# Another place in SBUF for x, and direct products of 512 columns cut in two

## The chip, the cores and the metric

The kernel runs on one core of one Trainium2 chip. A NeuronCore has TensorE (matmuls, with its own queue of weight loads), VectorE, ScalarE, GpSimd (POOL) and SyncE, which issues most DMAs. The metric is the device time of one execution in microseconds. The time before is 1766.88 us, the median of three runs (1766.7 to 1767.4).

## The reference

Two layers work on 512 tokens of width 1024, in float32. Each has an FFN, a mixer and a second FFN, and each of the three ends in a layer norm over the residual:

```python
for l in range(DEPTH):
    x = layer_norm(DEEPNORM_ALPHA * x + 0.5 * swiglu_ffn(x, ffn1_w_gu[l], ffn1_w_down[l]), ln1_g[l], ln1_b[l])
    x = layer_norm(DEEPNORM_ALPHA * x + hybrid_mixer(x, w_in[l], w_out[l], attn_sinks[l],
                                                     rope_cos, rope_sin, ret_cos, ret_sin), ln2_g[l], ln2_b[l])
    x = layer_norm(DEEPNORM_ALPHA * x + 0.5 * swiglu_ffn(x, ffn2_w_gu[l], ffn2_w_down[l]), ln3_g[l], ln3_b[l])
```

`swiglu_ffn` multiplies x by a 1024 x 5632 matrix, gates one half of the result with the SiLU of the other, and multiplies by a 2816 x 1024 matrix. `hybrid_mixer` projects x to queries, keys, values and gates, runs a windowed softmax attention over one half of the heads and a chunked retention over the other, and projects the result back.

## The kernel before

Every float32 product is made of three reduced-precision ones. `split` writes the rounded value (`hi`, ScalarE, L168) and the rest (`lo`, VectorE, L169) of an operand; `mm3` (L183 to L185) issues hi x hi, hi x lo and lo x hi into the same bank of PSUM. The second argument of `mm3` is the stationary operand, the third the moving one. In the profile a matmul is named out<-moving,stationary: `ps<-xh,uh` streams xh against weights uh.

x lies transposed in `xh` and `xl` (128 partitions, 8 blocks k of 512 tokens each). The weights arrive in two `raw` buffers of 8 KB per partition and are cut into units of 128 x 1024, `uh` and `ul`, six buffers each; `Weights` hands them out in order.

An FFN has eleven column pairs. Pairs 2 to 10 are `glu7`: seven products in place of eight by sums of quarters, so one pass has 72 matmuls with x as moving operand (`xb`) and 96 with sums of x as moving operand (`Th`, `Tl`, made once per FFN by `sums_of_x`), all of 256 columns. Pairs 0 and 1 are direct products through `proj` and `projs`: most are called for 256 tokens, the last two of pair 1 for all 512. Then the second matrix of the FFN is applied with tokens as output rows: `seventh` and `down` take parts of h, which `operand` splits into the room of xh and xl, as stationary operand and stream 512 columns of a unit. The last pair of h lies in `hr`, with units of its own at the tail.

The mixer projects with `emit_T` (256 tokens, the last call 512), `proj_tok` (x stationary, 512 columns of a unit streamed) and, for the retention, `projs` over 512 tokens. Attention and retention are tasks in Python generators that `step` runs between the products; `proj` yields where a step may come: behind half of the k blocks and at the end if it is called for 512 tokens, at the end alone otherwise. So TensorE's order is fixed when the program is written.

Tiles lie in pools, one pool behind the other, each tile padded to a multiple of 32 bytes. In the program before, `base` holds ident (512 bytes per partition, byte 2176), mhalf (32 bytes), xh (byte 2720), xl (19104) and Y (35488). Modulo 256 the last three are at 160. The raw buffers begin at 51872 (160) and the units at 68256 (160); each unit has 4096 bytes, and its eight blocks of 512 bytes lie at 160 too. Behind the units lies `small` (960 bytes in all: three st of 64, three mv, ve and rs of 32 each, and others), then at 118368 the pools of the FFN or the mixer: hT at 96, S and R at 96, Th at 179808 and Tl at 196192, both at 96, hr and the tail's units at 96; the mixer's tiles from qk on at 32.

Of the kernel before, what the change touches and what calls it, by code (L numbers as in the profile page):

```python
# [7 lines left out]
F32 = mybir.dt.float32  # L8
# [7 lines left out]
SEQ = 512  # L16
D = 1024
DFF = 2816
P = 128
KC = D // P  # L20
# [26 lines left out]
class Weights:  # L47


    def __init__(self, T, items):  # L50
        self.T, self.items = T, items
        self.emitted = self.taken = self.out = 0
        self.ready = []
        self.raws = {}
        self.last = {raw: i for i, (raw, _, _, _) in enumerate(items)}
# [44 lines left out]
class Trunk:  # L100
    def __init__(self, tc, ctx):
        self.tc, self.nc = tc, tc.nc
        self.n = 0
        self.now = 0
        self.pin = True
        self.tasks = []
        self.later = []
        self.pace = None
        self.halves = 2
        nc = self.nc  # L110
        self.base = ctx.enter_context(tc.tile_pool(name="base", bufs=1))
        self.rawp = ctx.enter_context(tc.tile_pool(name="rawp", bufs=2))
        self.unit = ctx.enter_context(tc.tile_pool(name="unit", bufs=UBUFS))
        self.small = ctx.enter_context(tc.tile_pool(name="small", bufs=3))
        self.psum = ctx.enter_context(tc.tile_pool(name="psum", bufs=8, space=PSUM))
        self.ident = self.base.tile([P, P], F32, name="ident")
        make_identity(nc, self.ident)
        self.mhalf = self.base.tile([P, 8], F32, name="mhalf")
        nc.vector.memset(self.mhalf, -0.5)
        self.xh = self.base.tile([P, KC, SEQ], F32R, name="xh")  # L120
        self.xl = self.base.tile([P, KC, SEQ], F32R, name="xl")
        self.Y = self.base.tile([P, NT, D], F32, name="Y")
# [320 lines left out]
    def proj(self, out, u, t0, t1):  # L443
        hv, lv = u
        for k in range(KC):
            self.mm3(out, (hv[:, k, :], lv[:, k, :]),
                     (self.xh[:, k, t0:t1], self.xl[:, k, t0:t1]), k == 0, k == KC - 1)
            if k == KC - 1 or (k == KC // 2 - 1 and t1 - t0 == SEQ):
                yield

    def projs(self, *args):
        for _ in self.proj(*args):
            self.step()

    def proj_tok(self, out, us, t):
        ts = slice(t * P, (t + 1) * P)
# [36 lines left out]
    def norm(self, t, halves, gb, out=None, delay=4, scale=(ALPHA, ALPHA)):  # L493
        nc = self.nc
        g, b = gb
        y = self.Y[:, t, :]
        st = self.small.tile([P, 2, 6], F32, tag="st", name=self.nm("st"))
        for h in range(2):
            hs = slice(h * 512, (h + 1) * 512)
            nc.vector.scalar_tensor_tensor(out=y[:, hs], in0=y[:, hs], scalar=scale[h], in1=halves[h],  # L500
                                           op0=ALU.mult, op1=ALU.add)
            nc.vector.bn_stats(out=st[:, h, :], in_=y[:, hs])
        mv = self.small.tile([P, 2], F32, tag="mv", name=self.nm("mv"))
        nc.vector.bn_aggr(out=mv, in_=st)
        ve = self.small.tile([P, 1], F32, tag="ve", name=self.nm("ve"))
        nc.vector.tensor_scalar_add(ve, mv[:, 1:2], LN_EPS)
        rs = self.small.tile([P, 1], F32, tag="rs", name=self.nm("rs"))
        nc.gpsimd.tensor_tensor(out=rs, in0=ve, in1=self.mhalf[:, 0:1], op=ALU.pow)
        nc.vector.scalar_tensor_tensor(out=y, in0=y, scalar=mv[:, 0:1], in1=g, op0=ALU.subtract, op1=ALU.mult)
        parts = [slice(0, D)] if out is None else [slice(0, 512), slice(512, D)]  # L510
        for hs in parts:
            nc.vector.scalar_tensor_tensor(out=y[:, hs], in0=y[:, hs], scalar=rs, in1=b[:, hs],
                                           op0=ALU.mult, op1=ALU.add)
            if out is not None:
                nc.sync.dma_start(out[t * P : (t + 1) * P, hs], y[:, hs])
        if out is None:
            self.pend.append(self.spawn(self.y_to_xT(t), delay))
# [670 lines left out]
```

## Time and profile before

| | |
|---|---|
| median of 3 runs | 1766.88 us |
| span of the profiled execution | 1765.1 us |
| TensorE busy | 1752.7 us (99%), 11930 matmuls |
| VectorE busy | 1414.9 us (80%) |
| ScalarE busy | 928.1 us (53%) |
| POOL busy | 182.9 us (10%) |

The profiled execution has a span, from the first to the last instruction, of 1765.1 us; the median of the runs is 1.8 us above it. Matmuls are pipelined: the durations in the profile overlap, so the sum over the groups is well above the span, and the time that a matmul takes of TensorE is seen in the distance of two starts in the timeline.

### The profile page before, as it was taken

How to read it: one execution, taken by the hardware profiler on the slowest of the kernel's cores; microseconds unless marked ns; L12 is line 12 of the kernel's file. 1: busy time of each engine (PE TensorE's matmuls, PEld its weight loads, DVE VectorE, ACT ScalarE, POOL GpSimd, SP SyncE). 2: the span in 40 equal slices, each digit the busy share in tenths (PEclk: the TensorE clock that was granted, in tenths of full speed). 3: DMA queues.
4: the chain of work that ended last, by engine and by line, in shares of the span. 5: the costliest groups of instructions: out<-in, count | busy, mean ns of one | idle time of the engine just before them, and what ended most of it. 6: DMA issues, size and time to landing. Idle time of an engine off the chain costs nothing.

```text
span 1765.1 us, 29166 instructions
## 1 busy us (share of the span) xinstructions
PE 1752.7 (99%) x11930; PEld 1600.5 (91%) x11930; DVE 1414.9 (80%) x1975; ACT 928.1 (53%) x1456; POOL 182.9 (10%) x152
## 2 busy tenths in 40 slices
PE   9999999999999999999999999999999999999998
PEld 9999988887789999998899999889877899999886
DVE  7888888856767888878888888888567587888887
ACT  5455556378712455555535555554795234555561
POOL 0000022111111000014000000311011110000131
PEclk9999999999999999999999999999999999999999
DMA  6234389422222243369423334982233122334891
GB/s 191 97 96 133 131 202 199 131 85 88 73 79 72 74 137 102 97 208 214 140 68 99 121 96 147 211 203 91 85 95 96 48 95 97 97 96 132 211 218 48
DMA packets 163765, 216.34 MB, mean 123 GB/s; under 512 B 5168, under 2 KB 116528, under 8 KB 163632
## 3 DMA queue, kind: packets, MB, share of 16 engines
q1 hardware_dynamic: 141872, 172.55, 30.5%
q0 software_dynamic: 21760, 41.95, 13.1%
q8 instruction: 93, 1.52, 0.3%
q14 instruction: 40, 0.33, 0.1%
HBM read 212.38 MB, written 2.10 MB: 122 GB/s over the span
## 4 chain that ended last, share of the span: by engine, by line
PE 90%; issue 6%; DMA 1%; DVE 1%; POOL 1%; ACT 0%; SPq 0%; POOLq 0%; DVEq 0%
PE ps L183 29%; PE ps L185 29%; PE ps L184 29%; PE ps L476 1%; DMA raw<-in_ffn_w_gu_dram 1%; POOL sw L959 1%; PE ps L1067 1%; PE ps L1015 0%; PE ps L1029 0%; PE ps L1063 0%; PE ps L1050 0%; DMA retS<-c_retS_dram 0%; ACT sw L957 0%; DVE ul L169 0%; PE ps L1007 0%
## 5 line engine op out<-in xcount | busy, mean ns | idle before, releaser
L183 PE MATMUL ps<-xh,uh 128*128 128x256 f32 (+1 forms) x1616 | 482.2, 298 | 0.0
L185 PE MATMUL ps<-xh,ul 128*128 128x256 f32 (+1 forms) x1616 | 479.3, 297 | 1.0 <-DVE ul L169 0.9
L184 PE MATMUL ps<-xl,uh 128*128 128x256 f32 (+1 forms) x1616 | 478.5, 296 | 0.3 <-DVE xl L169 0.3
L168 ACT CAST uh<-raw 128x1024 fp32r<-128x1024 f32 (+1 forms) x274 | 237.1, 886 | 245.6 <-PE ps L184 140.1
L169 DVE TENSOR_TENSOR ul<-raw,uh 128x1024 fp32r<-128x1024 f32 (+1 forms) x274 | 273.3, 1013 | 62.2 <-ACT uh L168 61.6
L183 PE MATMUL ps<-Th,uh 128*128 128x256 f32 x1152 | 319.1, 277 | 0.0
L184 PE MATMUL ps<-Tl,uh 128*128 128x256 f32 x1152 | 318.7, 277 | 0.0
L185 PE MATMUL ps<-Th,ul 128*128 128x256 f32 x1152 | 318.3, 276 | 0.0
L185 PEld LDWEIGHTS ps<-xh,ul 128*128 128x128 f32 x1616 | 307.9, 191 | 10.1 <-DVE ul L169 1.6
L183 PEld LDWEIGHTS ps<-xh,uh 128*128 128x128 f32 x1616 | 307.9, 191 | 9.7 <-issue 1.6
L184 PEld LDWEIGHTS ps<-xl,uh 128*128 128x128 f32 x1616 | 308.0, 191 | 7.9 <-DVE xl L169 0.5
L183 PE MATMUL ps<-uh,xh 128*128 128x512 f32 x720 | 283.4, 394 | 0.5 <-ACT xh L168 0.5
L185 PE MATMUL ps<-uh,xl 128*128 128x512 f32 x720 | 280.8, 390 | 0.0
L184 PE MATMUL ps<-ul,xh 128*128 128x512 f32 x720 | 280.3, 389 | 0.0
L168 ACT CAST uh<-S 128x1024 fp32r<-128x1024 f32 x144 | 151.1, 1049 | 149.0 <-PE ps L184 145.2
L169 DVE TENSOR_TENSOR ul<-S,uh 128x1024 fp32r<-128x1024 f32 x144 | 175.9, 1222 | 60.1 <-ACT uh L168 59.5
L184 PEld LDWEIGHTS ps<-Tl,uh 128*128 128x128 f32 x1152 | 216.7, 188 | 0.0
L183 PEld LDWEIGHTS ps<-Th,uh 128*128 128x128 f32 x1152 | 216.6, 188 | 0.0
L185 PEld LDWEIGHTS ps<-Th,ul 128*128 128x128 f32 x1152 | 216.4, 188 | 0.0
L389 POOL DMA_DIRECT2D R<-in_ffn_w_down_dram x80 | 97.1, 1217 | 1020.7 <-DVE ul L169 930.0
L169 DVE TENSOR_TENSOR ul<-R,uh 128x1024 fp32r<-128x1024 f32 x120 | 145.1, 1221 | 25.8 <-ACT uh L168 25.7
L183 PEld LDWEIGHTS ps<-uh,xh 128*128 128x128 f32 x720 | 135.2, 188 | 30.1 <-issue 1.6
(143 smaller groups left out, 2362.4 us busy)
## 6 DMA issues: line engine op xcount, KB each, us to landing
raw<-in_ffn_w_gu_dram SPq DMA_DIRECT2D x86, 1024.0 KB, 5.5
R<-in_ffn_w_down_dram POOLq DMA_DIRECT2D x80, 512.0 KB, 7.6
raw<-in_w_in_dram SPq DMA_DIRECT2D x18, 1024.0 KB, 5.2
R<-in_ffn_w_down_dram SPq DMA_DIRECT2D x16, 1024.0 KB, 6.3
raw<-in_ffn_w_down_dram SPq DMA_DIRECT2D x12, 1024.0 KB, 7.2
R<-in_ffn_w_down_dram SPq DMA_DIRECT2D x8, 512.0 KB, 4.3
raw<-in_w_in_dram SPq DMA_DIRECT2D x8, 512.0 KB, 6.1
raw<-in_w_out_dram SPq DMA_DIRECT2D x8, 512.0 KB, 6.4
```

What stands on the lines that cost most here:

```text
L168: a = self.nc.scalar.copy(hi, src)
L169: b = self.low = self.nc.vector.tensor_sub(lo, src, hi.bitcast(F32))
L183: keep(mm(out, ah, bh, start=start, stop=False, **kw))
L184: keep(mm(out, ah, bl, start=False, stop=False, **kw))
L185: keep(mm(out, al, bh, start=False, stop=stop, **kw))
L389: self.nc.gpsimd.dma_start(src, rows(i, j, g * 2, 2), accum_op=ALU.add))
L476: nc.tensor.transpose(b[:, c * P : (c + 1) * P], src[:, c * P : (c + 1) * P], self.ident)
L959: nc.gpsimd.tensor_mul(sw[:, :n], sw[:, :n], S)
L1067: ins = nc.tensor.matmul(ob[:, o0 : o0 + HD], ST[h][:, n, :], vr[:, n, p * P + h * HD : p * P + (h + 1) * HD], start=n == 0, stop=n == 0 o ...
```

## The change

Three tiles of 64 bytes are added to `base` ahead of xh; `norm` uses them in turn for its statistics, in place of tiles from `small`. A pool of one 64-byte tile is put between the raw buffers and the units. In `small`, st goes, ve becomes the third element of mv, and one tile of 32 bytes is added. The two new filler tiles are set to zero on GpSimd at the start. `proj` yields at its end alone, and `projs` calls it for 256 tokens at a time, with a step behind each.

```diff
         self.rawp = ctx.enter_context(tc.tile_pool(name="rawp", bufs=2))
+        self.near = ctx.enter_context(tc.tile_pool(name="near", bufs=1))
+        nc.gpsimd.memset(self.near.tile([P, 16], F32, name="apart"), 0.0)
         self.unit = ctx.enter_context(tc.tile_pool(name="unit", bufs=UBUFS))
         self.small = ctx.enter_context(tc.tile_pool(name="small", bufs=3))
         self.psum = ctx.enter_context(tc.tile_pool(name="psum", bufs=8, space=PSUM))
+        nc.gpsimd.memset(self.small.tile([P, 8], F32, tag="behind", name="behind", bufs=1), 0.0)
         self.ident = self.base.tile([P, P], F32, name="ident")
...
         nc.vector.memset(self.mhalf, -0.5)
+        self.stats = [self.base.tile([P, 2, 8], F32, name=f"st{i}") for i in range(3)]
+        self.norms = 0
         self.xh = self.base.tile([P, KC, SEQ], F32R, name="xh")
...
-            if k == KC - 1 or (k == KC // 2 - 1 and t1 - t0 == SEQ):
-                yield
-
-    def projs(self, *args):
-        for _ in self.proj(*args):
-            self.step()
+        yield
+
+    def projs(self, out, u, t0, t1):
+        for t in range(t0, t1, SEQ // 2):
+            for _ in self.proj(out[:, t - t0 : t - t0 + SEQ // 2], u, t, t + SEQ // 2):
+                self.step()
...
-        st = self.small.tile([P, 2, 6], F32, tag="st", name=self.nm("st"))
+        st = self.stats[self.norms % 3][:, :, :6]
+        self.norms += 1
...
-        mv = self.small.tile([P, 2], F32, tag="mv", name=self.nm("mv"))
-        nc.vector.bn_aggr(out=mv, in_=st)
-        ve = self.small.tile([P, 1], F32, tag="ve", name=self.nm("ve"))
+        mv = self.small.tile([P, 3], F32, tag="mv", name=self.nm("mv"))
+        ve = mv[:, 2:3]
+        nc.vector.bn_aggr(out=mv[:, :2], in_=st)
```

## Rows read from the trace of the kernel before

**Rows 1.** The page: span, TensorE's busy time, the chain by engine.
```profile
span 1765.1 us, 29166 instructions
...
PE 1752.7 (99%) x11930; PEld 1600.5 (91%) x11930; DVE 1414.9 (80%) x1975; ACT 928.1 (53%) x1456; POOL 182.9 (10%) x152
...
PE 90%; issue 6%; DMA 1%; DVE 1%; POOL 1%; ACT 0%; SPq 0%; POOLq 0%; DVEq 0%
```

**Rows 2.** Waits of TensorE, first and last of six: us in total, times, longest.
```profile
PE ps L468 <- POOL ident masks.py:199: 1.4, 1, 1.4
...
PE ps L184 <- DVE xl L169: 0.3, 1, 0.3
```

**Rows 3.** Groups by form on TensorE: shapes xcount | busy us, mean ns | idle.
```profile
L183 PE MATMUL ps<-xh,uh 128*128 128x256 f32 x1408 | 398.5, 283 | 0.0
...
L183 PE MATMUL ps<-Th,uh 128*128 128x256 f32 x1152 | 319.1, 277 | 0.0
...
L183 PE MATMUL ps<-uh,xh 128*128 128x512 f32 x720 | 283.4, 394 | 0.5 <-ACT xh L168 0.5
...
L183 PE MATMUL ps<-xh,uh 128*128 128x512 f32 x208 | 83.6, 402 | 0.0
```

**Rows 4.** One pass of glu7: us, busy of PE, PEld, DVE, ACT, POOL, PEclk, DMA.
```profile
111.62:131.14 19.52, 19.52 (x170) 19.52 (x170) 16.90 (x26) 10.62 (x18) 0.00 (x0) 1.00 0.35 109
```

**Rows 5.** Timeline of TensorE in that pass (start us, us), x before, T between.
```profile
113.20 0.29 PE L183 MATMUL ps<-Th,uh 128*128 128x256 f32 x1
...
113.56 0.28 PE L183 MATMUL ps<-Th,uh 128*128 128x256 f32 x1
...
115.94 0.28 PE L183 MATMUL ps<-xh,uh 128*128 128x256 f32 x1
```

**Rows 6.** Timeline of TensorE, a stretch on x alone.
```profile
12.30 0.28 PE L183 MATMUL ps<-xh,uh 128*128 128x256 f32 x1
...
16.26 0.28 PE L183 MATMUL ps<-xh,uh 128*128 128x256 f32 x1
```

**Rows 7.** Timeline of TensorE, 512 columns, x stationary, then hr stationary.
```profile
312.40 0.39 PE L185 MATMUL ps<-uh,xl 128*128 128x512 f32 x1
...
314.44 0.39 PE L185 MATMUL ps<-uh,xl 128*128 128x512 f32 x1
314.67 0.39 PE L183 MATMUL ps<-uh,hr 128*128 128x512 f32 x1
...
315.59 0.39 PE L184 MATMUL ps<-ul,hr 128*128 128x512 f32 x1
...
319.44 0.39 PE L183 MATMUL ps<-uh,hr 128*128 128x512 f32 x1
```

**Rows 8.** Timeline of TensorE, 512 columns behind a block of transposes.
```profile
329.66 0.40 PE L185 MATMUL ps<-uh,xl 128*128 128x512 f32 x1
329.90 0.39 PE L183 MATMUL ps<-uh,xh 128*128 128x512 f32 x1
...
331.27 0.39 PE L183 MATMUL ps<-uh,xh 128*128 128x512 f32 x1
```

**Rows 9.** Timeline of the start: a constant's memset, the second half's transposes.
```profile
0.24 0.10 POOL L1174 MEMSET const-float32-0.0<- 128x1 f32 x1 [0.24 <-issue]
0.27 0.10 POOL L1174 MEMSET const-float32-1.0<- 128x1 f32 x1
...
5.83 0.55 PE L476 MATMUL ps<-ident,Y 128*128 128x128 f32 x3 [0.30 <-DMA Y<-in_x_dram]
```

**Rows 10.** Timeline of TensorE, its longest idle behind the start.
```profile
23.07 0.39 PE L185 MATMUL ps<-xh,ul 128*128 128x256 f32 x1 [0.70 <-DVE ul L169]
```

**Rows 11.** Groups by form on VectorE: the splits of 128 x 1024.
```profile
L169 DVE TENSOR_TENSOR ul<-raw,uh 128x1024 fp32r<-128x1024 f32 x166 | 201.7, 1219 | 45.5 <-ACT uh L168 44.9
L169 DVE TENSOR_TENSOR ul<-S,uh 128x1024 fp32r<-128x1024 f32 x144 | 175.9, 1222 | 60.1 <-ACT uh L168 59.5
```

**Rows 12.** Groups by form on TensorE in the first 26.3 us.
```profile
L183 PE MATMUL ps<-xh,uh 128*128 128x256 f32 x41 | 11.8, 287 | 0.0
```

## The prediction

> **What bounds the kernel now.** I read the head of the page first: the span is 1765.1 us, TensorE is busy for 99% of it, and 90% of the chain that ended last runs through TensorE [rows 1]. Then the waits of TensorE: six kinds, 4.2 us in all, the longest of them the start of the program [rows 2]. So no other engine and no transfer holds this kernel back for long. TensorE always has a next matmul, and the time is the sum of the distances from one matmul's start to the next one's start. I call that distance the pitch. The durations in the groups by form [rows 3] are no pitch (a 256-column matmul is listed with 283 ns, and its successor starts long before that); a pitch is read from the timeline, as the difference of two starts divided by the matmuls between them.
>
> The timeline gives three pitches. A locked stretch on Th and Tl has 21 pitches from 113.56 to 115.94, so 113.3 ns each [rows 5]. A stretch on xh and xl has 33 from 12.30 to 16.26, so 120.0 ns [rows 6]. Both are 256 columns, the same weight units, the same three products of mm3, both back to back. What differs is where the moving operand lies: T at 96 modulo 256 bytes, x at 160, where the weight units are too. The third pitch, 512 columns of a unit with x (or hr) as stationary operand, is 227 ns (312.40 to 314.67, ten) or 226.5 ns (315.59 to 319.44, seventeen) [rows 7]. In all of these moving and stationary operand have the same offset: units and x both 160, the tail's units and hr both 96.
>
> A change of operand needs some matmuls to settle: the first three on T take 0.36 us, still 120 each, before the pitch falls to 113.3 [rows 5]. So a single pitch behind a change tells little of where the stream settles.
>
> **The change part by part.** *Placement.* Three 64-byte statistics tiles in base move xh, xl, Y and the raw buffers up by 192 bytes, to 96 modulo 256; 64 more bytes in front of the units put those back at 160. In `small` 192 + 96 bytes go and 32 come, so 256 less: what lies behind it (hT, S, T, all of the mixer) stays at its byte. After the change a product on x has the relation that T has now: moving 96, stationary 160.
>
> *256-column products on x.* There are 3 x 1408 = 4224 [rows 3]. 36 passes of glu7 (nine in each of four FFNs) hold 72 each beside 96 on T; one pass takes 19.52 us [rows 4]. With all 168 at 113.3 ns it takes 19.04 us, so 0.48 us less; times 36 that is 17.3 us. This includes T's settling, which has no cause any more when x and T lie alike. Outside the passes are 4224 - 2592 = 1632. Of these 41 + 2 x 40 = 121 start in the first 26.3 us [rows 12], where TensorE runs into weights that are still arriving (0.70 us at 23.07, behind a split) [rows 10]; faster matmuls only wait longer there, so I count nothing for them. 1511 x 6.7 ns = 10.1 us. Together 27.4 us.
>
> *What hides behind TensorE now.* In a pass VectorE is busy for 16.90 and ScalarE for 10.62 of 19.52 us [rows 4]. Both still fit into 19.04 us with 2.1 us to spare, so the splits don't become the bound. The raw buffers' new offset costs their readers nothing: VectorE's split takes 1219 ns from raw at 160 and 1222 ns from S at 96, each with units at 160 [rows 11].
>
> *512 as twice 256.* 3 x 208 = 624 direct products [rows 3] become 1248 of 113.3 ns: 226.6 ns in place of 226.5 to 227, so nothing. (What stays is a weight load more per pair, which TensorE hides at 113.3 ns already on T.) The tasks that are hung between are stepped once behind each half, as now behind half of the 24 matmuls: at the same times. The consumers (rotate, gate) read the whole bank after both halves, and the unit is released there, as before.
> [...]
>
> *512-column products with x as stationary operand.* The change doesn't name them, yet it moves one of their operands: in the seventh and proj_tok, 3 x 720 = 2160 matmuls [rows 3] stream a unit at 160 against x at 96. The trace has this relation only in single pitches at the border to hr, 0.23 us like the rest (314.44 to 314.67) [rows 7]. Bounds: below, the 6.7 ns between 120.0 and 113.3 could come off here too, 2160 x 6.7 = 14.4 us less; above, the mean of seven pitches behind a block of transposes, (331.27 - 329.66) / 7 = 230 ns [rows 8], 3.3 ns more than the settled pitch, 7 us more. I take zero: the settled pitch is 226.5 to 227 ns at two different offsets, and it equals two of the undisturbed 113.3, as if the pair that disturbs at 256 columns had room to spare at 512.
>
> *Small things.* Two memsets on POOL now precede the identity. The constants' memsets start 0.03 us apart and take 0.10 us; the first x block's second half of transposes waits for its transfer at 5.83 us [rows 9], so 0.1 to 0.2 us of delay is covered there, and if it weren't, it is 0.2 us. norm issues the same instructions; its ve now lies in mv's tile, and no new wait on another engine follows, since POOL reads ve alone and VectorE only reads mv behind it. The 192 transposes of Y (eight for each of 24 blocks) get their stationary operand at 96 too; at 6.7 ns each way that is 1.3 us more or less, which I leave at zero.
>
> *Sum.* The profiled execution has a span of 1765.1 us, 1.8 us under the median of 1766.88, so what lies around the span stays 1.8 us. 1766.9 - 27.4 = 1739.5 us.
>
> **The rivals.**
> *Stationary x gains too.* The extra time of a pitch would be a cost of each weight load against its stream, 6.7 ns whatever the columns; then 512 at unlike offsets settles at 220. [...] Against it: no settled 512 stretch under 226.5. Price -14.4 us: 1725 us.
> *Stationary x loses some.* The reversed relation (moving 160, stationary 96) isn't T's. If it holds the stream at the 230 of [rows 8] or a little over, it costs 7 to 15 us: 1747 to 1755 us.
> *Slower.* The single pitch of 0.24 us that stands in the same rows (329.66 to 329.90) [rows 8] becomes the settled one for the 2160, and then some: the break-even is 27.4 / 2160 = 12.7 ns, so a pitch of 239.4. At 240 the time is 1768; at 247, three steps of 6.7 over today's, it is 1783 us. Against it: no pitch in an undisturbed stretch stays there.
> *The change doesn't do what it says.* T may be faster for another reason than its offset: it lies near the upper end of SBUF, is read with 1024 bytes from one k to the next where x has 2048, and is written once per FFN. Then all of x stays at 120.0 and the time is 1766 to 1767 us.
> [...]
>
> **How the numbers follow.** Forecast (1736 to 1743 us) 50%; stationary x gains (1725) 15%; it loses some (1744 to 1760) 23%; the offset isn't the cause (1766 to 1767) 8%; slower (1771 and up) 4%. About 0.2%, 3.5 us, is what a measurement of this kernel can tell from no change. So faster 0.88, same 0.08, slower 0.04. The range reaches from the lower rival, 1724, to the upper part of the third case, 1756; outside are the last two cases and a little of the third.
>
> **What the profile after would show.** The 256-column form of xh,uh has 1824 instructions in place of 1408 (1408 + 2 x 208), the 512-column form on x as moving operand is gone, and TensorE counts 11930 + 624 = 12554 matmuls. A pass of glu7 takes 19.04 us; no settling shows between x and T, 21 pitches taking 2.38 us wherever they are counted. The 2160 matmuls with x stationary stand at 226 to 227 ns, which is the number to look at first if the total is off: each ns there is 2.2 us. A pass that stays at 19.52 means that the offset isn't what separates x from T. A pass between the two with TensorE idle would mean that the splits bind, against my step on VectorE.

## The result and the profile after

| | before | after |
|---|---|---|
| median | 1767.07 us (1766.7 to 1767.4) | 1779.33 us (1776.0, 1776.0, 1782.6, 1783.4) |
| ratio | | 1.0071, 95% interval 1.0052 to 1.0090 |
| profiled execution | span 1765.1 us | 1776.04 us, span 1774.3 us |
| TensorE busy, matmuls | 1752.7 us, 11930 | 1759.4 us, 12554 |

The forecast was 1739.5 us, 1724 to 1756. The change makes the kernel slower, and its runs stand on two levels some 7 us apart, where those of before agree within 0.7 us.

Page of after, its head (compare [rows 1]); then groups by form on TensorE (compare [rows 3]):

```profile
span 1774.3 us, 30416 instructions
...
PE 1759.4 (99%) x12554; PEld 1629.4 (92%) x12554; DVE 1416.0 (80%) x1975; ACT 928.3 (52%) x1456; POOL 181.6 (10%) x154
```
```profile
L188 PE MATMUL ps<-xh,uh 128*128 128x256 f32 x1824 | 513.4, 281 | 0.9 <-DVE b L988 0.7 <-ACT uh L173 0.2
...
L188 PE MATMUL ps<-Th,uh 128*128 128x256 f32 x1152 | 322.3, 280 | 0.0
...
L188 PE MATMUL ps<-uh,xh 128*128 128x512 f32 x720 | 285.2, 396 | 0.5 <-ACT xh L173 0.5
```

TensorE is still busy for 99%, with the 1824 and 12554 instructions that were forecast. But T, which the change doesn't touch, has gone up: 319.1 to 322.3 us. So most of the added time is pitch, in the sense of the prediction. Next, one pass of glu7 in each of the four FFNs of after (FFN 1 to 4, as they run; windows: stretch and its length, TensorE busy and its matmuls, granted clock, DMA share, GB/s; a count includes matmuls that reach over an end; compare [rows 4]):

```profile
113.70:132.74 19.04, 19.04 (x171) 1.00 0.34 111
637.88:657.67 19.79, 19.79 (x170) 1.00 0.33 105
971.80:991.58 19.78, 19.78 (x170) 1.00 0.33 107
1520.28:1540.06 19.78, 19.78 (x170) 1.00 0.33 108
```

The first FFN has exactly the 19.04 us of the forecast. The other three take 19.79 us for the same 168 matmuls, 0.27 us more than a pass before the change, at the same granted clock: 19.79 / 168 = 117.8 ns each, x and T alike. The start of such a stream, from the timeline of after, the second FFN:

```profile
564.17 0.38 PE L481 MATMUL ps<-ident,Y 128*128 128x128 f32 x2
564.31 0.36 PE L188 MATMUL ps<-xh,uh 128*128 128x256 f32 x1
564.51 0.28 PE L189 MATMUL ps<-xl,uh 128*128 128x256 f32 x1
564.63 0.28 PE L190 MATMUL ps<-xh,ul 128*128 128x256 f32 x1
564.75 0.28 PE L188 MATMUL ps<-xh,uh 128*128 128x256 f32 x1
```

Behind the transposes the stream is at 117.8 at once (0.12 from 564.51 on), and its 1800 matmuls stay there until it ends at 776 us. It does not settle to anything better.

Where the time went, as sums of all distances between starts, in us:

| | before | after | forecast of the difference | measured |
|---|---|---|---|---|
| x moving, and T | 1047.3 | 1047.7 | -27.4 | +0.4 |
| 2160 with x stationary | 495.1 | 499.2 | 0 | +4.1 |
| fp32 matmuls (attention, retention, transposes) | 103.1 | 107.5 | 0 | +4.4 |

The first line hides two opposite changes: x alone went from 653.6 to 644.5 us, and T, which stands where it stood, from 393.7 to 403.2 us. Of the 27.8 us missing in that line, three streams of 1800 at 117.8 for 113.3 are 5400 x 4.49 ns = 24.2 us.

### The profile page after: what moved, and what is told of

Its sections match the earlier page's. It is cut to its first block, busy times and chain, and to the rows that moved or that the text cites. A ratio compares the mean times of both kernels' runs of the same rounds, so it can differ in the third digit from the quotient of the medians.

```text
span 1774.3 us, 30416 instructions
## 1 busy us (share of the span) xinstructions
PE 1759.4 (99%) x12554; PEld 1629.4 (92%) x12554; DVE 1416.0 (80%) x1975; ACT 928.3 (52%) x1456; POOL 181.6 (10%) x154
## 4 chain that ended last, share of the span: by engine, by line
PE 92%; issue 3%; DVE 2%; ACT 2%; DMA 1%; POOL 0%; SPq 0%; POOLq 0%; DVEq 0%; ACTq 0%
PE ps L188 29%; PE ps L189 29%; PE ps L190 29%; PE ps L481 1%; DMA raw<-in_ffn_w_gu_dram 1%; PE ps L1073 1%; DVE b L988 1%; ACT b L1005 1%; ACT b L999 0%; DVE ul L174 0%; POOL sw L965 0%; ACT uh L173 0%; PE ps L1021 0%; PE ps L1035 0%; PE ps L1069 0%
## 5 line engine op out<-in xcount | busy, mean ns | idle before, releaser
L188 PE MATMUL ps<-xh,uh 128*128 128x256 f32 x1824 | 513.4, 281 | 0.9 <-DVE b L988 0.7
L190 PE MATMUL ps<-xh,ul 128*128 128x256 f32 x1824 | 510.3, 280 | 1.1 <-DVE ul L174 1.1
L189 PE MATMUL ps<-xl,uh 128*128 128x256 f32 x1824 | 510.2, 280 | 0.3 <-DVE xl L174 0.3
L188 PEld LDWEIGHTS ps<-xh,uh 128*128 128x128 f32 x1824 | 346.9, 190 | 4.1 <-issue 1.6
L189 PEld LDWEIGHTS ps<-xl,uh 128*128 128x128 f32 x1824 | 343.4, 188 | 0.8 <-DVE xl L174 0.5
L190 PEld LDWEIGHTS ps<-xh,ul 128*128 128x128 f32 x1824 | 342.6, 188 | 1.7 <-DVE ul L174 1.7
L188 PE MATMUL ps<-Th,uh 128*128 128x256 f32 x1152 | 322.3, 280 | 0.0
L189 PE MATMUL ps<-Tl,uh 128*128 128x256 f32 x1152 | 322.3, 280 | 0.0
L190 PE MATMUL ps<-Th,ul 128*128 128x256 f32 x1152 | 322.3, 280 | 0.0
L188 PE MATMUL ps<-uh,xh 128*128 128x512 f32 x720 | 285.2, 396 | 0.5 <-ACT xh L173 0.5
L188 PEld LDWEIGHTS ps<-Th,uh 128*128 128x128 f32 x1152 | 219.9, 191 | 0.0
L188 PEld LDWEIGHTS ps<-uh,xh 128*128 128x128 f32 x720 | 135.3, 188 | 32.2 <-issue 1.6
```

The lines of the kernel that those rows point to most:

```text
L188: keep(mm(out, ah, bh, start=start, stop=False, **kw))
L189: keep(mm(out, ah, bl, start=False, stop=False, **kw))
L190: keep(mm(out, al, bh, start=False, stop=stop, **kw))
```

## The experiments

A stream is an unbroken run of 256-column matmuls. Its way in is what TensorE ran just ahead of it.

Theory A: the pitch that a stream settles at depends on the offset of the moving operand against the stationary one; at the new difference two pitches are stable, 113.3 and 117.8 ns, and the way into the stream chooses. Theory B: the offset alone sets the pitch, and something else that happens in the later FFNs holds them back.

**Map of offsets, other engines idle.** Only copies x out and runs 128 chains of 48 matmuls; no layer is computed.

```python
for s0 in (0, 8):                     # elements: stationary offset
    for N in (256, 512):
        for m0 in range(0, 64, 8):    # moving offset, steps of 32 bytes
            for e in range(4):        # four ways in
                ...
                chain(B[n % 8], 48, N, m0, s0)
```

> This kernel leaves the reference's work out: it copies x to the output and runs 128 chains of 48 matmuls on TensorE, each chain with one offset of the moving operand against the stationary one (eight steps of 32 bytes, the stationary operand at 224 and at 0 modulo 256), 256 or 512 columns, entered in four ways (four plain float32 matmuls, then none or three short ones of 80, 96 or 112 columns). Theory A, two settled pitches: at some offsets the pitch that a chain settles at depends on the way in; with the moving operand 64 bytes below the stationary one chains of 256 columns settle at 113.3 ns or at 117.8 ns, at equal offset all of them at 120.0 ns. Theory B, the offset alone sets the pitch and the 117.8 ns of the changed kernel come from what the other engines do in the later FFNs: here, with the other engines idle, every chain with 64 bytes below settles at 113.3 ns. Both expect 226.7 ns for 512 columns at equal offset and about 229 ns with the moving operand 64 bytes above (three pitches of 229, 232, 226).

Windows over the last 27 pitches of six chains: 256 columns at equal offset, then twice at a difference of 192 with two ways in; 512 columns at 0, 64 and 192:

```profile
665.40:668.64 3.24, 3.24 (x30) 1.00 0.00 0
829.50:832.56 3.06, 3.06 (x30) 1.00 0.00 0
836.25:839.43 3.18, 3.18 (x29) 1.00 0.02 5
907.92:914.04 6.12, 6.12 (x28) 1.00 0.00 0
1005.57:1011.75 6.18, 6.18 (x28) 1.00 0.01 3
1202.60:1208.90 6.30, 6.30 (x29) 1.00 0.00 0
```

3.24 / 27 is 120.0 ns; 3.06 and 3.18 us are 113.3 and 117.8 ns, for the same instructions on the same addresses, with nothing else running. All chains, settled, in ns (eight for each cell; the program's very first chain left out), by moving minus stationary offset modulo 256 bytes:

| | 0 | 32 | 64 | 96 | 128 | 160 | 192 | 224 |
|---|---|---|---|---|---|---|---|---|
| 256 columns | 120.0 | 116.7 to 117.8 | 117.8 (7), 113.3 (1) | 119.9 to 120.1 | 118.6 to 120.0 | 117.4 to 120.0 | 113.3 (6), 117.8 (2) | 118.2 to 118.3 |
| 512 columns | 226.7 | 233.3 | 228.9 (6), 233.3 (2) | 233.3 | 232.1 to 233.5 | 234.2 to 234.4 | 233.2 to 233.4 | 233.3 to 233.4 |

As far as two stationary offsets can show, the difference counts and not the place: both keep within these ranges. (At 192 one of them gave 113.3 with all four ways in, the other with two.) 256 columns reach 113.3 at 64 and 192 alone, and not in each chain; 512 columns are best at equal offset. In the changed kernel x against a unit is 96 - 160, so 192; a unit against stationary x is 64.

**Placement alone**, the 512-column products kept.

```diff
-    def projs(self, out, u, t0, t1):
-        for t in range(t0, t1, SEQ // 2):
-            ...
+            if k == KC - 1 or (k == KC // 2 - 1 and t1 - t0 == SEQ):
+                yield
```

> The changed placement alone; direct products on x keep their 512 columns. Theory A: each FFN's long stream of 256-column products takes one of the two settled pitches, 113.3 or 117.8 ns, and keeps it through all nine passes (19.04 or 19.79 us per pass); which one may differ from FFN to FFN and from run to run, in steps of about 7 us of the whole. Theory B: the first FFN at 113.3 and the other three at 117.8, in every run. The 512-column products with x as moving operand show what they cost at unlike offsets; at 226.7 ns the cut in two is worth nothing, at 230 or more the 624 of them cost 2 us or more against two halves of 113.3.

Measured: 1755.19 us (1751.2, 1751.8, 1758.6, 1758.9), 0.9939 of before (0.9916 to 0.9961): faster than both kernels. Theory B's line for this run (the first FFN at 113.3, the others at 117.8) is not what the profile shows. A pass in FFN 1 and in FFN 2, and then the 48 products of 512 columns ahead of the first long stream, 11.19 / 48 = 233 ns each:

```profile
113.55:132.59 19.04, 19.04 (x171) 1.00 0.35 111
634.60:653.64 19.04, 19.04 (x170) 1.00 0.35 111
```
```profile
45.23:56.42 11.19, 11.19 (x50) 1.00 0.44 143
```

All four long streams stand at 113.3 here. They begin behind the 512-column products, and not behind transposes in one unbroken run as after the cut. With x stationary, 512 columns settle at 228.9, as the map has it for 64 (720 of L188 are busy for 285.2 us, as in after; before it was 283.4). The profiled run is on the lower level; the upper one, two runs of four, has no profile.

**The cut alone**, x left at 160.

```diff
-            if k == KC - 1 or (k == KC // 2 - 1 and t1 - t0 == SEQ):
-                yield
+        yield
...
+        for t in range(t0, t1, SEQ // 2):
```

> The cut alone; x stays at 160 as the units. Both theories: a 256-column product on x at equal offset settles at 120.0 ns, so the 624 direct products of 512 columns cost 240 in place of 226.7 ns: 8.3 us more, 1775 us. The passes of glu7 stay at 19.52 us and all runs lie within 1 us of each other.

Measured: 1776.07 us, 1.0050 (1.0035 to 1.0065). A pass stays at 19.52 us. 624 matmuls of 226.7 became 1248 of 120.0, which is 8.3 us; the sums give 7.1 more on x and 2.6 more on the fp32 matmuls.

```profile
117.42:136.94 19.52, 19.52 (x171) 1.00 0.34 107
```

**Another way in.** The changed kernel, with twelve matmuls at equal offset (a unit's columns streamed past the same unit) ahead of the first glu7 pass of each FFN.

```diff
+            def nudge(u):
+                b_ = self.ps()
+                for k in range(4):
+                    v = [t[:, 2 * k : 2 * k + 2, :] for t in u]
+                    self.mm3(b_[:, :256]..., (u[0][:, k, :], u[1][:, k, :]), v, k == 0, k == 3)
...
+                    nudge(u1)
```

> The changed kernel with twelve more matmuls per FFN, between the pairs 0 and 1 and the passes of glu7: a unit as moving operand, 256 columns, against itself, both at 160, into a bank that nobody reads. Before the change every stream on T that came from 120.0 ns at equal offset settled at 113.3. Theory A: so do the long streams now, in all four FFNs and in every run: passes of 19.04 us; the three FFNs at 117.8 gain 3 x 1512 x 4.5 ns = 20 us, the twelve cost 4 x 1.4 us: about 1761 us, all runs within 1 us. Theory B: the passes of the later three FFNs stay at 19.8 us and the time rises by 6 us to 1782 us.

Measured: 1761.14 us (1760.95 to 1763.14), 0.9969 (0.9956 to 0.9982). With 48 matmuls more the kernel is 15 us faster than the lower level of after, as 3 x 1512 x 4.49 ns less the time of the added ones gives (18 us from median to median, which mixes the two levels of after). A pass in FFN 1 and FFN 2:

```profile
115.04:134.08 19.04, 19.04 (x170) 1.00 0.35 111
639.25:658.29 19.04, 19.04 (x170) 1.00 0.35 112
```

Every other instruction of the later FFNs is as in after, with the same neighbours on the other engines, so theory B falls. The 288 matmuls of FFN 2 that run ahead of the twelve still stand at 117.8; here are the last 287:

```profile
565.92:599.72 33.80, 33.80 (x289) 1.00 0.30 95
```

FFNs 3 and 4 show the same. In FFN 1 the stream came to the twelve at 113.3 already.

**What leads from one pitch to the other, other engines idle.** No layer is computed; first finer offsets, then 24 matmuls at 192, something in between, and 48 more at 192.

```python
for kick in KICKS:                    # e.g. [(12, 256, 8)]: 12 at equal offset
    for e in range(4):                # four ways in
        fresh(e); go(24, 256, S0 + 48)
        for c, N, m0 in kick: go(c, N, m0)
        go(48, 256, S0 + 48)
```

> This kernel leaves out the whole computation: it copies x to the output and runs chains of matmuls of 256 columns with the other engines idle. Part one, 17 differences of the moving operand's offset to the stationary one's, 16 bytes apart where the first map had 32. Theory A (the settled pitch is a matter of that difference, and where two are possible of the way in): the pitches lie between their neighbours' in the first map, 113.3 or 117.8 near 64 and 192 and 117 to 120 elsewhere, and no difference has 113.3 alone. Part two, at a difference of 192: 24 matmuls from four ways in, then something in between, then 48 more. Theory A: behind 12 or 24 matmuls at equal offset the 48 settle at 113.3 from each way in (the run with 12 ahead of each long stream did so in four of four); behind 3 or 6 not always; behind two chains of unequal columns (128 and 384, 192 and 320, and so on) each pair has its own outcome, for which I have no number. Rival B (the pitch is set by the offset and by other engines' work, not by the way in): all 52 chains of 48 come out alike, at 113.3, since no other engine works.

The differences of 8 to 248 bytes in steps of 16 all settle at 116.7 to 121.3 (the chain right behind the copies left out), so no better place lies between those of the map. Of the 52 chains of the second part:

| in between | the 48 settle at 113.3 | at 117.8 |
|---|---|---|
| 3, 6, 12 or 24 at equal offset | 16 of 16 | 0 |
| 224 + 288, 288 + 224, 384 + 128 columns | 12 of 12 | 0 |
| 128 + 384 | 3 | 1 |
| 512, or 272 + 240 | 4 | 4 |
| 320 + 192 | 1 | 3 |
| 192 + 320, 240 + 272 | 0 | 8 |

In the 16 chains of the first row the 24 matmuls ahead stood at 117.8 at their end, so what came in between changed the pitch. Rival B's line, all alike, is wrong. 512 columns lead either way, so nothing assures the entries that the placement alone had in its profile.

**Stationary h at the units' offset.** Placement alone, with h written 64 bytes further on. In three FFNs the last of h then lies over a few columns of the new x, so that part of x is lost; the instructions are the same.

```diff
+        self.hrooms = [t[:, 16:].rearrange("p (k c) -> p k c", k=KC) for t in (high, low)]
...
-                hh, hl = (v[:, k : k + f, ...] for v in (self.xh, self.xl))
+                hh, hl = (v[:, k : k + f, ...] for v in self.hrooms)
```

> The kernel with x's place changed but 512 columns kept (1755.19 us, its runs near 1751.5 and 1758.7), with h, the stationary operand of the second matrices' products, written 64 bytes further on in the same tiles, so that it lies at 160 as the units that stream past it; small tiles move to fill the room. Theory A (the difference of the offsets sets the pitch): the 1680 products of the FFNs with h in x's room settle at 226.67 ns in place of 228.89, 3.7 us less, all else alike: 1751.5 us in the median, with runs near 1747.8 and 1755. Rival C (512 columns over x's room settle at 229 because of where ScalarE and VectorE write meanwhile, not because of the difference): they stay at 229, and the time at 1751 to 1759.

The 336 products of the first FFN, after and here:

```profile
233.39:310.30 76.91, 76.91 (x338) 1.00 1.02 220
```
```profile
232.78:308.94 76.16, 76.16 (x337) 1.00 1.02 223
```

76.91 / 336 = 228.9 and 76.16 / 336 = 226.7 ns: theory A's size, and rival C falls. The profiled execution took 1747.58 us, where 1747.8 was expected. The median is 1755.22, where 1751.5 was expected and placement alone has 1755.19, over a wide spread (1747.6 to 1770.2), which no profile here explains; steps of 7 to 8 us in it are what one more long stream at 117.8 would cost, but that is only argued.

**The changed kernel once more.**

> The changed kernel as it is, profiled once more: its runs lay at 1776.0 and at 1783.0. Theory A: if this profile falls on the upper level, one of the long streams of the four FFNs that ran at 113.3 (the first FFN's, 1800 matmuls) runs at 117.8, and 1800 x 4.5 ns = 8.1 us is the whole of the 7 us between the levels; on the lower level the first FFN's stream is at 113.3 again and the other three at 117.8. Rival C: the levels come from elsewhere (DMA, the clock), and all four streams stand as in the first profile at either level.

It took 1774.58 us, the lower level, and stands as before: FFN 1 at 19.04, FFN 2 at 19.79 us. That agrees with A and does not decide about the upper level.

```profile
112.35:131.39 19.04, 19.04 (x170) 1.00 0.35 110
636.45:656.24 19.79, 19.79 (x171) 1.00 0.32 106
```

**Three matmuls, earlier.** The changed kernel, a single `mm3` at equal offset ahead of the second 256 tokens of pair 0.

```diff
+    def kick(self, out, u):
+        v = [t[:, 0:2, :] for t in u]
+        self.mm3(out[:, :256]..., (u[0][:, 0, :], u[1][:, 0, :]), v, True, True)
...
+                if first:
+                    self.kick(a, au[0])
```

> The changed kernel with three matmuls more in each FFN, at equal offsets (a unit's columns streamed past the same unit, 160 and 160), ahead of the second 256 tokens of pair 0; their result is overwritten. Theory A (two settled pitches at a difference of 64 or 192, the way in chooses, and three matmuls at equal offset lead into 113.3, as in 16 of 16 chains with such matmuls between): the streams of 1776 matmuls behind them run at 113.3 in all four FFNs; against the lower level of the changed kernel (1776.0) three FFNs gain 1776 x 4.49 ns = 8.0 us each, and the added matmuls cost 12 x 0.12 = 1.4 us: 1753.4 us, and no second level 7 us above. Rival B (FFNs 2 to 4 run at 117.8 for the sake of other engines' work): 1777.4 us, with the levels kept. Rival D (three are too few in this kernel, twelve are needed as in the run with 1761.1): between the two, with some of the four streams at 117.8.

A miss: 1776.47 us (1776.1 to 1784.1), 1.0055. The profile, of the run at 1784.13, shows the way in, the three between 574.39 and 574.74, and passes in FFN 1 and 2:

```profile
574.27 0.28 PE L190 MATMUL ps<-xh,ul 128*128 128x256 f32 x1
574.39 0.28 PE L188 MATMUL ps<-uh 128*128 128x256 f32 x1
574.51 0.28 PE L189 MATMUL ps<-ul,uh 128*128 128x256 f32 x1
574.62 0.28 PE L190 MATMUL ps<-uh,ul 128*128 128x256 f32 x1
574.74 0.28 PE L188 MATMUL ps<-xh,uh 128*128 128x256 f32 x1
```
```profile
116.41:136.20 19.79, 19.79 (x171) 1.00 0.33 107
645.41:665.20 19.79, 19.79 (x171) 1.00 0.33 107
```

The three take 0.35 us, under 120 ns each, so they don't reach the 120.0 of equal offset, and the stream goes on at 117.8, as the other three do in this profile. The run on the upper level has the first FFN at 19.79 too, where after on the lower level has 19.04; that has the size of the 8 us between the levels.

**Twelve in the same place.** The only difference to the last one:

```diff
-        self.mm3(out[:, :256]..., (u[0][:, 0, :], u[1][:, 0, :]), v, True, True)
+        for k in range(4):
+            v = [t[:, 2 * k : 2 * k + 2, :] for t in u]
+            self.mm3(o, (u[0][:, k, :], u[1][:, k, :]), v, k == 0, k == 3)
```

> The changed kernel with twelve matmuls at equal offset in the place where the run before had three (ahead of the second 256 tokens of pair 0); there none of the four streams behind them left 117.8. Theory A, mended (two settled pitches; what leads into 113.3 for certain is the settled pitch of 120 ns at equal offset, which three matmuls don't reach: in the run with twelve they stood at 120 when they ended): FFNs 2, 3 and 4 run their 1776 at 113.3, 3 x 7.9 us less, for 12 x 3 more matmuls of 0.12 us, 4.3 us more: against the run with three, 1776.2 on its lower level, 1756.8 us. The first FFN waits for weights right behind this place and keeps its two levels (1756.8 and 1764.8). Rival D (it was the place, or what ran beside it, not the number): 1780.5 us, all streams of FFNs 2 to 4 at 117.8.

Measured: 1756.70 us (1756.4 to 1757.9), 0.9944 (0.9929 to 0.9959); 1756.8 was expected. Rival D falls: with all else equal, the number decides in this kernel. FFN 1 and FFN 2:

```profile
113.46:132.50 19.04, 19.04 (x171) 1.00 0.35 112
636.48:655.52 19.04, 19.04 (x170) 1.00 0.35 113
```

No run is on the upper level, which I had still expected. In FFNs 2 to 4 the matmuls just ahead of the twelve stand at 117.8. In FFN 1 they are at 113.3 already, so there this profile shows only that the twelve keep it.

**Put together.** Placement; 512 columns cut in the FFNs and kept in the mixer; h at 160; three matmuls at equal offset in each FFN.

```diff
+                room = self.hrooms
+                if out is None and calls[0] >= 18:
+                    room, k, h = (self.xh, self.xl), (0, 4)[calls[0] % 2 == 0], 1
```

> Put together from what the runs gave: x at 96 and the units at 160; 512 columns of x kept in the mixer and cut in two in the FFNs; the three matmuls at equal offset in each FFN; h written at 160, except the last three of its operands in the three FFNs behind which x is written anew (in the run with all of h at 160 these overwrote part of x). Theory A: from 1751.5 (the lower level of x's place alone), 1620 matmuls with h stationary at 226.67 for 228.89 give 3.6 us, 192 products of 512 columns at 226.7 for 233.3 give 1.3, some 168 matmuls ahead of the long stream at 113.3 for 117.8 in three FFNs 2.3, and the twelve added ones take 1.4: 1745.7 us, between 1744 and 1748, without a second level. Rival B: 1751 to 1759, as x's place alone has it.

Measured: 1743.50 us (three of four runs at 1743.4 to 1743.6, one at 1750.7), 0.9879 (0.9859 to 0.9898): a little below the 1744 to 1748 of theory A, and with the second level that it excluded. The profiled run is the one at 1750.7, with FFN 1 at 117.8 and FFN 2 at 113.3:

```profile
115.81:135.60 19.79, 19.79 (x171) 1.00 0.33 108
638.49:657.53 19.04, 19.04 (x170) 1.00 0.35 112
```

FFN 1 changed its pitch on the way. Its stream came to the three at 113 ns (16 matmuls in 1.81 us). Right behind them two starts lie 0.30 and 0.23 us behind the ones before, and from there it runs at 117.7 (100 in 11.77 us):

```profile
22.69:24.50 1.81, 1.81 (x18) 1.00 0.08 14
25.60:37.37 11.77, 11.77 (x101) 1.00 0.20 67
```

In the first profile of after, with nothing added, the stream changes the other way at this place, at a wait of TensorE: 20 matmuls in 2.35 us ahead of it, near 117.8 each, and 100 in 11.33 us, 113.3 each, behind it:

```profile
23.74:26.09 2.35, 2.35 (x22) 1.00 0.12 31
26.66 0.38 PE L189 MATMUL ps<-xl,uh 128*128 128x256 f32 x1 [0.29 <-DVE xl L174]
27.00:38.33 11.33, 11.33 (x103) 1.00 0.27 85
```

So this stream changed its pitch at a wait, of 0.29 us at 26.66, and the first FFN has one at its start.

The same **without the added matmuls** (`self.kick(a, au[0])` taken out):

> The version put together, without its three added matmuls in each FFN. In its profile FFN 2 and FFN 4 came to that place at 117.8 and left it at 113.3, FFN 3 came and left at 113.3. Theory A: without them FFNs 2 and 4 stay at 117.8 through 1776 matmuls, 2 x 7.9 us more, less 1.4 us for the matmuls: 1743.4 + 14.4 = 1757.8 us, and 7 us more where the first FFN is at 117.8 too. Rival E (the added matmuls do nothing here, the streams are led into 113.3 by something else of this version): 1742.0 us.

Measured: 1758.50 us (six of eight runs at 1757.8 to 1758.6, two at 1765.3 and 1766.1), where 1757.8 was expected. The four FFNs:

```profile
113.60:132.64 19.04, 19.04 (x170) 1.00 0.34 110
633.97:653.76 19.79, 19.79 (x170) 1.00 0.34 109
983.33:1002.37 19.04, 19.04 (x170) 1.00 0.33 112
1523.58:1543.37 19.79, 19.79 (x171) 1.00 0.33 107
```

FFNs 2 and 4 are at 117.8, FFN 3 isn't, as forecast. So rival E falls: here three matmuls did lead those two over, as in the chains and unlike in the run with three alone. Fewer than the settled 120 may or may not do, and why is open.

**The same with twelve in the first FFN** and three in the others (`self.kick(a, au[0], 1 if self.norms else 4)`):

> The version put together (1743.5 in the median, one run at 1750.7 in whose profile the first FFN's stream ran at 117.9), with twelve matmuls at equal offset in the first FFN and three in the others. Theory A: twelve lead the first FFN's stream into 113.3 too, as in the run with twelve, for 9 x 0.12 = 1.1 us: 1744.5 us, all runs within 2 us, and four streams of 1776 at 113.3 in the profile. If the first FFN's level comes from elsewhere: 1744.5 with some runs at 1752.

Measured: 1743.82 us (1743.5 to 1744.7), 0.9869 (0.9852 to 0.9885), on one level in four runs. It beats before by 23.8 us and the median of after by 35.5 us (32 us its lower level). In FFN 1 the stream came to the twelve at 113.3 here too, and kept it. In the three kernels with twelve in FFN 1 none of 13 runs is on an upper level, against two of four of after. Four FFNs:

```profile
113.61:132.65 19.04, 19.04 (x171) 1.00 0.35 110
631.76:650.80 19.04, 19.04 (x170) 1.00 0.35 112
957.21:976.25 19.04, 19.04 (x171) 1.00 0.34 113
1494.41:1513.45 19.04, 19.04 (x171) 1.00 0.35 112
```

## Why the prediction was wrong

- *The bound, and pitches as the measure*: right. The whole result is a sum of pitches, and VectorE, at 16.88 us in a pass of 19.04 us of after, never binds in one.
- *"After the change a product on x has the relation that T has now"*, and so T's pitch: the step that failed. The relation is T's, but a relation doesn't have one pitch. T always settled at 113.3 in before (all 108 stretches of T in its profile) because each of its stretches came out of twelve or more matmuls on x at equal offset, and that way in led to 113.3 wherever a run had it (nine profiled streams of nine behind twelve, and eight chains of eight behind 12 or 24). The rows showed this entry, [rows 5], three pitches of 120 ahead of the 113.3; I read it as settling, a cost that would go away. It was what chose the pitch, and the change took it away along with the 120. In its place the second to fourth FFN came out of transposes, at 117.8.
- *The glu7 passes* (17.3 us): 0.48 us less in each pass of FFN 1 as worked out, 0.27 us more in each of the other three. With the way in mended (the run with twelve), all four have the forecast's 19.04.
- *512 as twice 256, "nothing"*: mis-sized in three ways. Two halves cost 226.7 only at 113.3; at 117.8 they cost 235.6. The cut joins the products into streams of 1800 that begin behind transposes: without it the four streams of the placement alone were at 113.3 in the profile. And the tasks are not stepped "at the same times": in the mixer TensorE now waits for VectorE's results, 2.5 us at L1035 where the same line (L1029 of before) had 0.8 us, part of the 4.4 us more on the fp32 matmuls. The cut brings that: the same sum is 102.3 us with the placement alone and 105.7 with the cut alone. Waits of TensorE in after (us, times, longest):

```profile
PE ps L1035 <- DVE qk L964: 1.5, 2, 0.8
...
PE ps L1035 <- DVE rr L1038: 1.0, 2, 0.5
```

- *The price of the cut*: the cut alone cost 9.2 us (1776.07 against 1766.9), and two halves against one of 512 have no single price. The map has twice 120.0 against 226.7 at equal offset, 13.3 ns for a pair, and twice 113.3 against 233.3 at 192, where two halves are the cheaper.
- *Stationary x, "I take zero"*: outside of zero, inside the bounds. Settled 228.9 for 226.7; 4.1 us by the sums against -14.4 to +7. That is the mechanism of the second rival, below its price. The run with h at 160 gives the 2.2 ns back. The reason given for zero, one pitch at two offsets, compared two places at the same difference (160 and 160, 96 and 96), so it said nothing of an unlike one.
- *The rivals*: none had two pitches at one relation. *Slower* has 1779 among its times (1768 at a pitch of 240, 1783 at 247), but its cause did not come: it puts the time on the 2160 with x stationary, which settled at 228.9. "The offset isn't the cause" is refuted by the map: with the other engines idle, 256 columns take 113.3 to 120.1 ns and 512 take 226.7 to 234.4 by offset.
- *What would show it*: a pass above 19.52 with TensorE always busy was not on my list.

What stays open: why a stream keeps 117.8 for 1800 matmuls, and what in a block of transposes, a wait or three matmuls chooses. The same block led FFNs 2 and 4 to 117.8 and FFN 3 to 113.3 in the run without added matmuls. The levels of the changed kernel are tied to FFN 1 by profiles of two kernels that differ in three matmuls for each FFN, not by both levels of one kernel.

## What to carry to other kernels

Before taking a pitch over from one stream to another, look at what each stream came out of: here the same shape at the same offsets held two speeds, 113.3 and 117.8 ns, and the change that removed the slow neighbour removed the fast entry. When TensorE is the bound, compare the pitch at the same place in each repeat of a loop; a mean hides that three of four repeats went the other way. Runs on two levels are worth a profile each: the step between them (7 to 8 us) is near the price of one stream (1800 x 4.49 ns = 8.1 us).

## What the runs showed of the hardware

- In the map, at its two stationary offsets, the pitch of back-to-back matmuls of this form (reduced-precision float32, 128 x 128 stationary, a weight load for each) went by moving minus stationary offset modulo 256 bytes: 120.0 ns at 0 and 113.3 or 117.8 at 64 and 192 for 256 columns; 226.7 at 0, 228.9 or 233.3 at 64, 233.3 at 192 for 512.
- At 192 a stream kept the pitch that it had: in after 117.8 ns over the 1800 matmuls of each of three FFNs, and 113.3 over the 1773 of the first FFN from 27.00 us on, through changes of unit, bank and moving tile, at a granted clock of 1.00.
- Behind twelve matmuls at equal offset all nine profiled streams stood at 113.3; six of them had come at 117.8, three at 113.3. So the same work with 48 matmuls more was 15 us faster, level against level (1761.1 against 1776.0).
- At a wait of TensorE a stream's pitch changed as well: from 117.8 to 113.3 ns, behind 0.29 us of waiting at 26.66 us in the first FFN of after.
